# Adding the squares on VectorE, with fewer and later tiny sums, and giving the order of the opening wave of a macaron layer by hand

## The chip, the core and the metric

The kernel runs on one core of one Trainium2 chip. A core has engines that each work through their own instructions in order: TensorE (PE in the profile, with its weight loads as PEld), VectorE (DVE), ScalarE (ACT), GpSimd (POOL), and SyncE (SP), which here only issues DMAs. The metric is the device time in microseconds (us). Three runs of the kernel before gave 2667.14, 2667.64 and 2669.3 us.

## The reference

```
h  = modulate(rms_norm(s, g), shift, scale)          # rms_norm(s) * g * (1 + scale) + shift
s += 0.5 * gate * (silu(h @ w_gate) * (h @ w_up)) @ w_down
```

This half feed-forward step, over 256 latent and 256 context tokens of 2048 features with 5632 hidden features, stands at the beginning and at the end of the layer; attention and a long convolution stand between. The shift, scale and gate of each step are `silu(c) @ w_ada + b_ada`, one vector of 2048 for the latent tokens and one for the context tokens. The convolution's filters come from a small sine network over positions, and are normalised and taken to the frequency domain; they depend on no token. Every large product is made from a high and a low part of each operand, as three products: high x high, high x low, low x high.

## The kernel before

The change lies in the first 170 us. Tokens run along the free axis and features along the partitions, so the input is 16 "d-tiles" of 128 features by 512 tokens (256 of each stream).

**Opening.** SP loads the input as 16 tiles of 256 KB (L547; each holds two d-tiles of one stream). ScalarE squares a tile as it arrives (L592), VectorE squares three of them (L585) and adds neighbours in pairs, and PE multiplies the squares by a matrix of ones (L603), 4 products of 2 columns for each pair and for each of the two last tiles, 36 in all; they are called the tiny sums here. Products of a constant by ones that nobody reads (`keep_awake`, L576) stand ahead of them and between them; an fp32 product of PE is recorded as two passes, so the first `keep_awake(8)` shows as 16. From the sums come 1/rms (L262 to L271), a diagonal matrix of it (L296) and a product that spreads it over the partitions (L297).

**Rows and columns.** Shift and scale of a d-tile are made on PE: a "row" of 16 products by `w_ada` (L174), a copy by ScalarE (L181), two transposes (L183), and on VectorE a reduction (L186) and four operations on single columns (L188, L190). A row needs two loads of 1 MB (`wrow`, L161); the pool holds four such tiles, so that the loads of row d+2 can start when row d has been read.

**Wave.** The normalised input of a d-tile is made by `wave_h`: scale times 1/rms (L622, VectorE), shift (L624, ScalarE, which rounds to the high part), and the low part (L626, VectorE). Three hidden tiles are then accumulated over the 16 d-tiles: a "tile" in the code is the 18 products of one d-tile (L232, L233, L234), 6 for each of the three. Round d holds row d+1, the transposes for d+1, and tile d. Weights of four d-tiles come at a time; their high part is cast by ScalarE (L221), their low part made by VectorE (L225), three of each for rounds 4 to 7, 8 to 11 and 12 to 15. In the kernel before they are cast at the head of rounds 4, 8 and 12.

**Filters.** `filter_spectrum` is a generator that the rounds advance three times each. It makes three sine layers (PE L436; VectorE L438 to L443; ScalarE L445), and then for each of four groups: exponentials (ScalarE, L467), a split of the last weights (L469, L470), the first filter products (PE L474, L475), their products with the exponentials (L476), sums and differences (L481, L482), absolute values (ScalarE, L486), their sum (L488, L489), the normaliser (PE L492, L493, then a reciprocal, L495), the transform (PE L501, VectorE L502 to L507), and two stores that ScalarE's queue issues (L509).

**Order.** A scheduling layer decides the order of each engine from the program and the marks `issue_after` (in `then`), which say behind which instruction another may be placed. What is not marked, it places where it expects it to be ready. At run time each engine's order is fixed. After the wave, 41 more hidden tiles and the rest of the layer follow.

Of the kernel before, what the change touches and what calls it, by code (L numbers as in the profile page):

```python
# [18 lines left out]
P = 128  # L19
# [17 lines left out]
AWAKE = (8, 3, 4)  # L37
# [18 lines left out]
def hybrid_layer_kernel(ctx: ExitStack, tc: tile.TileContext, a):  # L56
# [58 lines left out]
    mod = [[None] * 9, [None] * 9]  # L115
    for c in range(9):
        for i in range(2 if c < 5 else 1):
            mod[i][c] = T(const, (P, KT), f"mod{i}_{c}")
# [58 lines left out]
    def ada_col(d):  # L177
# [9 lines left out]
        for i in range(2):  # L187
            V.scalar_tensor_tensor(mod[i][1][:, d : d + 1], col[:, 0, i : i + 1], bada1[:, d : d + 1], gn[:, 0, d : d + 1],  # L188
                                   op0=ALU.add, op1=ALU.mult)
            V.tensor_add(mod[i][0][:, d : d + 1], col[:, 1, i : i + 1], bada[:, d : d + 1])  # L190
# [221 lines left out]
    def filter_spectrum():  # L412
# [20 lines left out]
        for li in range(3):  # L433
# [13 lines left out]
            if li == 0:  # L447

                mats = U((P, 2, 2, P))
                nc.sync.dma_start(mats, a["fdft"])  # L450
                taps = [load_taps(0)]
# [118 lines left out]
    def keep_awake(n, behind=None, bank=spin):  # L570

        with ExitStack() as order:
# [9 lines left out]
    step = None  # L582
# [4 lines left out]
    for n, t in enumerate(xs[0] + xs[1]):  # L587
        i, sq = n // 8, U((P, 2, L))
        if n in (5, 8, 11):
# [5 lines left out]
        if n < 14 and n % 2 == 0:  # L595
            prior = sq
            continue
        if n < 14:
            step = vector(V.tensor_add, sq, prior, sq)
        for tt in range(2):  # L600
            for j in range(2):
                with tc.issue_after(awake.ins):
                    last = PE.matmul(sums[:, 2 * i + tt, :], sq[:, j, tt * P : (tt + 1) * P], ones[:, 0:2],  # L603
                                     start=(n, tt, j) == (1, 0, 0), stop=(n, tt, j) == (15, 1, 1))
                awake = last
        if n in (3, 7, 11):
            awake = keep_awake(1, awake)
# [7 lines left out]
    with tc.issue_after(spread_mm[-1].ins):  # L615
        ada_row(0, (1,))

# [16 lines left out]
    with tc.issue_after(roots[-1].ins):  # L634
        made = first_hi(0, head)
    with tc.issue_after(made.ins):
        copied, turned_, bank = ada_col(0)
    keep_awake(AWAKE[1], turned_, bank)
    with tc.issue_after(spread.ins):
        made = [first_hi(j, head) for j in range(1, WAVE)][-1]  # L640
    with tc.issue_after(made.ins):
        shifted, lo_last = wave_h(0)
    with tc.issue_after(lo_last.ins):
        for j in range(WAVE):
            first_lo(j, head)
# [9 lines left out]
    def col_on(d):  # L655
        if d < KT:
            ada_col(d)
            wave_h(d)

    firsts = []  # L660
    for d in range(KT):
# [755 lines left out]
```

## Time and profile before

| | us |
|---|---|
| median of three runs | 2667.64 |
| the profiled execution's own time | 2666.05 |
| its span, from the first to the last instruction | 2664.3 |
| PE busy in the span | 2642.3 |
| VectorE busy | 1721.9 |
| ScalarE busy | 939.1 |
| mean granted TensorE clock | 0.996 |

A row of the timeline gives start, duration, engine, line, operation, output <- inputs, sizes, and how many instructions it merges; in brackets stands how long the engine was idle before, and what ended that. In a row of the stage windows stand the stage, its length, the busy time of PE, PEld, DVE, ACT and POOL with their instruction counts, the granted clock as a share of full speed, the busy share of the DMA engines, and GB/s. PE's records overlap, so that its busy time says less than the distance between starts.

### The profile page before, as it was taken

How to read it: one execution, taken by the hardware profiler on the slowest of the kernel's cores; microseconds unless marked ns; L12 is line 12 of the kernel's file. 1: busy time of each engine (PE TensorE's matmuls, PEld its weight loads, DVE VectorE, ACT ScalarE, POOL GpSimd, SP SyncE). 2: the span in 40 equal slices, each digit the busy share in tenths (PEclk: the TensorE clock that was granted, in tenths of full speed). 3: DMA queues.
4: the chain of work that ended last, by engine and by line, in shares of the span. 5: the costliest groups of instructions: out<-in, count | busy, mean ns of one | idle time of the engine just before them, and what ended most of it. 6: DMA issues, size and time to landing. Idle time of an engine off the chain costs nothing.

```text
span 2664.3 us, 32528 instructions
## 1 busy us (share of the span) xinstructions
PE 2642.3 (99%) x12522; PEld 2176.8 (82%) x12522; DVE 1721.9 (65%) x2727; ACT 939.1 (35%) x1236; POOL 7.3 (0%) x19
## 2 busy tenths in 40 slices
PE   9999999999999999999999999999999999999999
PEld 6578888888888888888888988888788888888887
DVE  4779899986596767543434597789765555554444
ACT  3333222222222222222222465457454444444333
POOL 0000000000000000000000000000000000000000
PEclk8999999999999999999999999999999999999999
DMA  9876656665686566622222355335555555556664
GB/s 353 306 270 221 228 211 221 214 228 206 227 294 237 206 226 213 229 95 100 98 95 95 135 174 190 127 121 166 180 176 189 190 189 189 189 190 206 203 200 158
DMA packets 145686, 515.77 MB, mean 194 GB/s; under 512 B 16699, under 2 KB 21756, under 8 KB 141180
## 3 DMA queue, kind: packets, MB, share of 16 engines
q1 hardware_dynamic: 142460, 504.13, 55.1%
q0 software_dynamic: 1296, 4.72, 0.5%
q10 hardware_dynamic: 1776, 4.85, 0.5%
q8 instruction: 98, 1.61, 0.2%
q14 instruction: 56, 0.46, 0.1%
HBM read 509.43 MB, written 4.21 MB: 193 GB/s over the span
## 4 chain that ended last, share of the span: by engine, by line
PE 97%; DVE 1%; DMA 1%; ACT 1%; SPq 0%; issue 0%; DVEq 0%; ACTq 0%
PE pa L232 12%; PE pa L233 12%; PE pa L234 12%; PE pa L1080 10%; PE pa L1081 10%; PE pa L1079 10%; PE pb L232 7%; PE pb L233 7%; PE pb L234 7%; PE pa L240 3%; PE pa L242 2%; PE pa L793 1%; PE pa L794 1%; PE pa L792 1%; PE pb L174 1%; DMA wrow<-in_w_ada_dram 0%
## 5 line engine op out<-in xcount | busy, mean ns | idle before, releaser
L225 DVE TENSOR_TENSOR wlo<-raw,whi 128x1024 fp32r<-128x1024 f32 x639 | 781.4, 1223 | 649.2 <-ACT whi L221 642.8
L221 ACT CAST whi<-raw 128x1024 fp32r<-128x1024 f32 x639 | 672.3, 1052 | 1342.7 <-PE pa L233 485.9
L232 PE MATMUL pa<-u,whi 128*128 128x512 f32 x1376 | 535.3, 392 | 6.6 <-ACT u L624 6.4
L233 PE MATMUL pa<-u,whi 128*128 128x512 f32 x1376 | 536.7, 390 | 0.0
L234 PE MATMUL pa<-u,wlo 128*128 128x512 f32 x1376 | 535.7, 389 | 0.0
L1079 PE MATMUL pa<-whi,u 128*128 128x512 f32 x1060 | 413.9, 391 | 0.0
L1080 PE MATMUL pa<-wlo,u 128*128 128x512 f32 x1060 | 412.8, 390 | 0.2 <-DVE wlo L225 0.2
L1081 PE MATMUL pa<-whi,u 128*128 128x512 f32 x1060 | 412.8, 390 | 0.0
L232 PEld LDWEIGHTS pa<-u,whi 128*128 128x128 f32 x1376 | 258.2, 188 | 65.0 <-ACT u L624 8.4
L233 PEld LDWEIGHTS pa<-u,whi 128*128 128x128 f32 x1376 | 258.5, 188 | 55.0 <-issue 1.2
L234 PEld LDWEIGHTS pa<-u,wlo 128*128 128x128 f32 x1376 | 258.5, 188 | 53.5
L232 PE MATMUL pb<-u,whi 128*128 128x512 f32 (+1 forms) x800 | 298.5, 373 | 0.0
L233 PE MATMUL pb<-u,whi 128*128 128x512 f32 (+1 forms) x800 | 298.1, 373 | 0.0
L234 PE MATMUL pb<-u,wlo 128*128 128x512 f32 (+1 forms) x800 | 297.5, 372 | 0.0
L1081 PEld LDWEIGHTS pa<-whi,u 128*128 128x128 f32 x1060 | 199.0, 188 | 41.4
L1080 PEld LDWEIGHTS pa<-wlo,u 128*128 128x128 f32 x1060 | 199.1, 188 | 41.3 <-DVE wlo L225 0.6
L1079 PEld LDWEIGHTS pa<-whi,u 128*128 128x128 f32 x1060 | 199.0, 188 | 40.8
L137 DVE CUSTOM_DVE_ANT_0 adas<-adaw,crow,mod 128x1024 bf16<-128x1024 f32 x160 | 205.1, 1282 | 17.1 <-DMA adaw<-in_w_adaT_dram 14.1
L137 DVE CUSTOM_DVE_ANT_0 adas<-adaw,crow,cond 128x1024 bf16<-128x1024 f32 x160 | 204.8, 1280 | 15.5 <-DMA adaw<-in_w_adaT_dram 13.8
L232 PEld LDWEIGHTS pb<-u,whi 128*128 128x128 f32 x800 | 150.6, 188 | 27.2 <-issue 0.9
L233 PEld LDWEIGHTS pb<-u,whi 128*128 128x128 f32 x800 | 150.7, 188 | 26.8 <-issue 0.8
L234 PEld LDWEIGHTS pb<-u,wlo 128*128 128x128 f32 x800 | 150.7, 188 | 26.1
(277 smaller groups left out, 2136.1 us busy)
## 6 DMA issues: line engine op xcount, KB each, us to landing
raw<-in_w_up_dram SPq DMA_DIRECT2D x340, 512.0 KB, 3.3
adaw<-in_w_adaT_dram SPq DMA_DIRECT2D x223, 512.0 KB, 4.7
raw<-in_w_dn_dram SPq DMA_DIRECT2D x184, 512.0 KB, 3.4
wrow<-in_w_ada_dram SPq DMA_DIRECT2D x32, 1024.0 KB, 8.3
raw<-in_w_hy_dram SPq DMA_DIRECT2D x32, 512.0 KB, 3.3
raw<-in_w_o_dram SPq DMA_DIRECT2D x32, 512.0 KB, 3.4
raw<-in_w_kv_dram SPq DMA_DIRECT2D x16, 512.0 KB, 3.2
raw<-in_w_q_dram SPq DMA_DIRECT2D x16, 512.0 KB, 3.3
```

The costliest lines, as they stand in the source:

```text
L137: V.tensor_tensor_reduce(out=sc, in0=t, in1=crow[i][:, b * (D // 2) : (b + 1) * (D // 2)], scale=1.0, scalar=mcol if b else bada[:, n : n ...
L174: last = PE.matmul(bank[g : g + 32, 0 : 2 * P], cs[:, k, :], t[:, k8, :], start=k < 4, stop=k >= KT - 4)
L221: S.copy(hi, raw)
L225: V.tensor_sub(lo, raw, hi.bitcast(F32))
L232: PE.matmul(ps, w[0], xx[0], start=start, stop=False)
L233: PE.matmul(ps, w[0], xx[1], start=False, stop=False)
L234: return PE.matmul(ps, w[1], xx[0], start=False, stop=stop)
L240: PE.matmul(ps, w[0], x, start=start, stop=stop)
L242: PE.matmul(ps[:, 0, :], w[1], x[:, 0, :], start=False, stop=False)
L1079: PE.matmul(ps[t], hi, w[0], start=start, stop=False)
L1080: PE.matmul(ps[t], hi, w[1], start=False, stop=False)
L1081: last = PE.matmul(ps[t], lo, w[0], start=False, stop=stop)
```

## The change

1. **Squares.** ScalarE squares 15 tiles, VectorE only tile 14. VectorE adds tiles 0 to 7 into one and 8 to 13 into another. The tiny sums are 16 instead of 36: of the first sum, of the second, and of tiles 14 and 15.
2. **`keep_awake`.** 32 products at the start instead of 8, 14 behind the first tiny sums instead of three single ones, none behind the transposes of d-tiles 0 and 1 (3 and 4 before).
3. **1/rms ahead.** For d-tiles 0 and 1, VectorE multiplies the input by 1/rms beforehand (`times_rs`), and ScalarE applies scale and shift at once (`wave_h_early`); VectorE makes the same again and subtracts the high part.
4. **Columns.** Shift and scale of both streams of a d-tile are written by two operations on two columns instead of four on one.
5. **Order of a round.** Each tile, row and pair of transposes is marked to stand behind the one before: row d+1, the first third of tile d, the transposes, the other two thirds. The filter's products stay unmarked, between them.
6. **Weights.** The casts for rounds 4, 8 and 12 are written behind the thirds of rounds 3, 7 and 11.
7. **Filter loads.** The loads of the first group (`taps`) stand one sine layer later.

```diff
-AWAKE = (8, 3, 4)
+AWAKE = (32, 0, 0, 14)
...
-        if n in (5, 8, 11):
+        if n == 14:
...
-        if n < 14 and n % 2 == 0:
-            prior = sq
+        if n < 14 and n % 8:
+            step = vector(V.tensor_add, acc, acc, sq)
+        if n in (7, 13):
+            sq = acc
+        elif n < 14:
+            acc = acc if n % 8 else sq
             continue
-        if n < 14:
-            step = vector(V.tensor_add, sq, prior, sq)
...
-        if n in (3, 7, 11):
-            awake = keep_awake(1, awake)
+        if n == 7:
+            awake = keep_awake(AWAKE[3], awake)
...
+    def times_rs(d):
+        early[d] = U((P, 2, L))
+        for i in range(2):
+            last = V.tensor_mul(early[d][:, i, :], xd(i, d), rs[:, i, :])
+        return last
+    def wave_h_early(d):
...
+            shifted = S.activation(hi[:, i, :], t[:, i, :], AF.Identity, bias=mod[i][0][:, d : d + 1],
+                                   scale=mod[i][1][:, d : d + 1])
...
+            V.tensor_scalar(t[:, i, :], t[:, i, :], mod[i][1][:, d : d + 1], mod[i][0][:, d : d + 1],
+                            op0=ALU.mult, op1=ALU.add)
+        last = V.tensor_sub(lo, t, hi.bitcast(F32))
...
+    def weights_on(d, j):
+        if d % 4 == 3 and d + 1 < KT:
+            w[j] = weight(None, (P, 4, 2, P), raw=raws[j])
...
+    for d in range(1, KT):
         if d > 1:
-            then(mm, row_on, d + 1)
+            mm = then(mm, row_on, d + 1) or mm
         for j in range(WAVE):
-            if d and d % 4 == 0:
-                w[j] = weight(None, (P, 4, 2, P), raw=raws[j])
-            mm = f1.tile(d, d % 4, w[j], wave[j])
+            mm = then(mm, f1.tile, d, d % 4, w[j], wave[j])
...
+            if j == (1 if d == 1 else 0):
+                mm = then(mm, col_on, d + 1) or mm
+            weights_on(d, j)
+            if (d, j) != (1, 0):
                 next(steps, None)
```

The lines of the changed kernel lie by one or two below those of the kernel before in the generator (its L475 is L474 before); `keep_awake` is L578, the tiny sums L607, the 1/rms products L628, `wave_h_early` L635 to L640, `wave_h` L648 to L652.

**PE, the program's start.** Before, from the seventh row of PE on (`u` the squares or the constant, `pb_171` the sums, `pb_267` row 0):

```order
L576 MATMUL pa_170<-u_74,ones_72 128x256
L603 MATMUL pb_171<-ones_72,u_221 128x2 x4
L603 MATMUL pb_171<-ones_72,u_230 128x2 x4
L576 MATMUL pa_170<-u_74,ones_72 128x256
L603 MATMUL pb_171<-ones_72,u_240 128x2 x4
L603 MATMUL pb_171<-ones_72,u_247 128x2 x4
L603 MATMUL pb_171<-ones_72,u_253 128x2 x4
L174 MATMUL pb_267<-wrow_142,csp_76 32x256 x8
L297 MATMUL pb_277<-sg_276,ones_72 128x512
L174 MATMUL pb_267<-wrow_144,csp_76 32x256 x8
L183 MATMUL pb_267<-ident_67,sg_296 128x128 x2
L576 MATMUL pb_267<-u_74,ones_72 128x256 x3
```

In the changed kernel, from PE's first product on:

```order
L578 MATMUL pa_167<-u_74,ones_72 128x256 x32
L607 MATMUL pb_168<-ones_72,u_201 128x2 x4
L578 MATMUL pa_167<-u_74,ones_72 128x256 x14
L607 MATMUL pb_168<-ones_72,u_243 128x2 x4
L607 MATMUL pb_168<-ones_72,u_264 128x2 x4
L607 MATMUL pb_168<-ones_72,u_270 128x2 x4
L175 MATMUL pb_284<-wrow_139,csp_76 32x256 x8
L297 MATMUL pb_294<-sg_293,ones_72 128x512
L175 MATMUL pb_284<-wrow_141,csp_76 32x256 x8
L184 MATMUL pb_284<-ident_67,sg_321 128x128 x2
```

All 46 idle products now stand ahead of the last 12 tiny sums, and none behind the transposes.

**VectorE in round 4.** Before, the last sine layer (L442, L443), the weights (L225) and the reduction of row 5 (L186):

```order
L442 SCALAR_TENSOR_TENSOR mt_573<-mt_574,mt_573 128x256
L225 TENSOR_TENSOR wlo_636<-raw_468,whi_635 128x1024
L443 TENSOR_SCALAR mt_573<-mt_573 128x256
L225 TENSOR_TENSOR wlo_682<-raw_470,whi_681 128x1024
L626 SCALAR_TENSOR_TENSOR u_594<-sq_595,mod_0_6_83,u_593 128x256
L626 SCALAR_TENSOR_TENSOR u_594<-sq_595,mod_0_7_84,u_593 128x256
L457 TENSOR_TENSOR u_645<-u_582,u_645 64x256
L225 TENSOR_TENSOR wlo_701<-raw_472,whi_700 128x1024
L186 TENSOR_REDUCE col_99<-pb_614 128x4
```

In the changed kernel, at the same place (row 5 is `pb_628`):

```order
L442 SCALAR_TENSOR_TENSOR mt_597<-mt_598,mt_597 128x256
L187 TENSOR_REDUCE col_96<-pb_628 128x4
L442 SCALAR_TENSOR_TENSOR mt_597<-mt_598,mt_597 128x256
L188 SCALAR_TENSOR_TENSOR mod_6_83<-col_96,bada_17_95,cond_78 128x2
L442 SCALAR_TENSOR_TENSOR mt_597<-mt_598,mt_597 128x256
L190 TENSOR_SCALAR mod_6_83<-col_96,cond_78 128x2
L443 TENSOR_SCALAR mt_597<-mt_597 128x256
```

The sine layer's last operations have moved from ahead of row 5's reduction to behind it.

**PE and VectorE at the end of round 7.** PE before, from the end of tile 7 on (`pb_955` is the second group's normaliser, `wrow_905` row 9):

```order
L234 MATMUL pb_294<-u_843,wlo_701 128x512
L174 MATMUL pb_888<-wrow_814,csp_76 32x256 x8
L174 MATMUL pb_888<-wrow_816,csp_76 32x256 x8
L183 MATMUL pb_888<-ident_67,sg_921 128x128 x2
L232 MATMUL pa_289<-u_930,whi_983 128x512
L232 MATMUL pa_290<-u_930,whi_983 128x512
L492 MATMUL pb_955<-u_865,ones_72 128x256
L493 MATMUL pb_955<-u_915,u_165 1x256
L174 MATMUL pb_962<-wrow_905,csp_76 32x256 x8
```

PE in the changed kernel, where row 8 and its transposes stand earlier in round 7 (row 9 is `wrow_901`):

```order
L233 MATMUL pb_311<-u_830,whi_624 128x512
L234 MATMUL pb_311<-u_829,wlo_625 128x512
L493 MATMUL pb_961<-u_861,ones_72 128x256
L494 MATMUL pb_961<-u_931,u_162 1x256
L175 MATMUL pb_968<-wrow_901,csp_76 32x256 x8
```

VectorE there, in the changed kernel, right behind the reduction of row 8 and its two small steps:

```order
L648 SCALAR_TENSOR_TENSOR sq_920<-u_115,mod_6_83,u_166 128x256
L648 SCALAR_TENSOR_TENSOR sq_920<-u_131,mod_6_83,u_166 128x256
L225 TENSOR_TENSOR wlo_928<-raw_789,whi_927 128x1024
L652 SCALAR_TENSOR_TENSOR u_919<-sq_920,mod_6_83,u_918 128x256 x2
L482 TENSOR_TENSOR u_931<-u_861 128x256
L483 TENSOR_TENSOR u_931<-u_861 128x256
L482 TENSOR_TENSOR u_934<-u_863 128x256
L483 TENSOR_TENSOR u_934<-u_863 128x256
L225 TENSOR_TENSOR wlo_944<-raw_791,whi_943 128x1024
L489 TENSOR_TENSOR u_861<-u_861,u_863 128x512
L225 TENSOR_TENSOR wlo_958<-raw_793,whi_957 128x1024
L490 TENSOR_TENSOR u_861<-u_861 128x256
```

PE's normaliser product has moved to the end of round 7, ahead of row 9; what makes its operand (L490) is the last of a chain on VectorE that begins with row 8's reduction and holds all three low parts of the weights.

More of the change, by code (lines that the diff above doesn't have):

```diff
@@ L570, in keep_awake @@
     def keep_awake(n, behind=None, bank=spin):
+        last = behind
         with ExitStack() as order:
@@ L581, in hybrid_layer_kernel @@
     awake = keep_awake(AWAKE[0])
-    step = None
+    step, acc = None, None
     def vector(do, *args):
@@ L653, in row_on @@
             return row
[L655 to L661, printed above, removed]
+    def weights_on(d, j):
+        if d % 4 == 3 and d + 1 < KT:
+            w[j] = weight(None, (P, 4, 2, P), raw=raws[j])
+    for j in range(WAVE):
+        mm = f1.tile(0, 0, w[j], wave[j]) if j == 0 else then(mm, f1.tile, 0, 0, w[j], wave[j])
+    with tc.issue_after(shifted.ins), tc.issue_after(lo_last.ins):
+        for j in range(2):
+            first_hi(j, rest)
+            first_lo(j, rest)
+        scaled = times_rs(1)
```

80 lines of the change are left out of this document (39 added, 41 removed).

## The prediction

> **What bounds the kernel now.** I read the page first, then busy time and clock by stages, then PE's waits, then the timeline of the stage that waits.
>
> ```profile
> 12.70:26.20 13.50, 13.28 (x64) 10.23 (x67) 3.38 (x10) 4.55 (x9) 0.00 (x0) 0.50 1.03 407
> ...
> 57.00:60.30 3.30, 3.20 (x19) 1.74 (x20) 0.00 (x0) 0.37 (x1) 0.00 (x0) 0.50 1.02 422
> ...
> 101.40:108.10 6.70, 5.25 (x33) 2.52 (x37) 4.41 (x8) 0.91 (x2) 0.00 (x0) 0.50 0.48 198
> ...
> 167.40:2664.20 2496.80, 2487.91 (x11510) 2072.79 (x11510) 1615.87 (x2446) 874.26 (x1121) 0.00 (x0) 1.00 0.54 185
> ```
>
> From 167.4 us on PE is busy for 2487.9 of 2496.8 us at the full clock. The change touches nothing behind that, so it can move the end only by moving the moment at which the wave ends. Ahead of it the clock is granted at half in three stretches: around the tiny sums, and behind 57 and 101 us.
>
> ```profile
> PE pa L232 <- ACT u L624: 6.4, 5, 3.3
> PE pb L174 <- DMA wrow<-in_w_ada_dram: 2.5, 1, 2.5
> PE pb L183 <- ACT sg L181: 1.6, 3, 0.6
> ```
>
> Up to 250 us PE's products wait 6.4 us for the wave's input (L624), 2.5 us once for row 4's load, and 1.6 us for copies. These, the half clock and the opening are what can be won.
>
> ```profile
> 1.25 5.94 PE L576 MATMUL pa<-u,ones 128*128 128x256 f32 x16 [1.25 <-POOL u L91]
> 8.41 1.05 PE L603 MATMUL pb<-ones,u 128*128 128x2 f32 x8 [0.43 <-DVE u L255]
> ...
> 16.84 5.12 PE L603 MATMUL pb<-ones,u 128*128 128x2 f32 x24
> ...
> 24.05 2.08 PE L297 MATMUL pb<-sg,ones 128*128 128x512 f32 x2 [0.22 <-DVE sg L296]
> ...
> 28.30 0.17 DVE L186 TENSOR_REDUCE col<-pb 128x4 f32<-128x16 f32 x1 [4.31 <-PE pb L183]
> 28.53 1.56 PE L576 MATMUL pb<-u,ones 128*128 128x256 f32 x6 [0.34 <-DVE col L186]
> ...
> 30.39 0.97 PE L232 MATMUL pa<-u,whi 128*128 128x512 f32 x3 [0.30 <-ACT u L624]
> ...
> 38.10 1.99 PE L576 MATMUL pb<-u,ones 128*128 128x256 f32 x8
> 39.79 0.77 PE L232 MATMUL pa<-u,whi 128*128 128x512 f32 x2
> ...
> 67.84 0.96 PE L232 MATMUL pa<-u,whi 128*128 128x512 f32 x3 [0.94 <-ACT u L624]
> ...
> 72.33 0.61 PE L474 MATMUL pb<-u,u 128*128 128x512 f32 x2
> ...
> 167.47 0.50 PE L232 MATMUL pa<-u,whi 128*128 128x512 f32 x1 [0.15 <-ACT sg L369]
> ```
>
> The marks I use: the tiny sums end at 21.96 (16.84 + 5.12), tile 0 starts at 30.39, tile 1 at 39.79, tile 4 ends at 72.33, and the wave at 167.2, just ahead of the last row. All times below are on this profiled execution's clock.
>
> **The opening.** It gets longer. Eight warm passes of an idle product take 1.99 us and six 1.56, so one takes 0.215. The first 16 took 5.94 where 16 warm ones would take 3.4: about 2.4 us went to a cold start. In the changed kernel 64 passes stand first: 1.25 + 64 x 0.215 + 2.4 = 17.4 us. The first eight tiny passes (1.05 us in the row with the tail of the last, 0.9 apart) bring 18.3, the 28 idle passes 6.0 more, 24.3, the last 24 tiny ones 2.7: 27.0. The additions on VectorE (0.7 us each, following the arrival of the tiles) are done by about 16 and are covered by this. Warm sums do save: 24 passes cost 5.12 at half clock. But they end 5.0 us later than before, because the 46 idle products cost more than the clock returns.
>
> From the end of the sums to the spreading product it took 2.09 us (21.96 to 24.05), so it starts at 29.1 and, warm, takes half of its 2.08. From its end to the reduction it took 2.17 (26.13 to 28.30): 32.3; on VectorE the new 1/rms products and three small low parts stand ahead, five operations of about 0.42 from 30.7 on, so I take 32.7. From reduction to tile 0 it was 2.09; without two column steps and the scaling product (together 0.6) it is 1.5. Tile 0 starts at 34.2, 3.8 later. The next such stretch, tile 0 to tile 1, took 9.40 and loses the same 0.6; the four idle products taken away there were inside this wait. Tile 1 starts at 43.0.
>
> A rule of the Trainium skill bears on this, "TensorE: Matmul & The Clock Gate", in its part on the HAM clock gate: a free-running window of 3.4 us in which PE is busy opens the clock, an idle one halves it. By PE's busy column the 13.50 us stretch above is busy for 13.28 and should have run at the full clock; the row shows 0.50, so tiny sums did not count as busy here, and the measurement decides. By the rule as it reads, the sums before would have cost half and the new opening would lose some 7 us instead of 5.
>
> **Rounds 1 to 4.** From tile 1 to the end of tile 4 it took 32.5 us before. The filter loads now stand behind row 4's, so the 2.5 us wait goes, and with it the half clock of 57.00 to 60.30, which cost 1.65. With the weights cast a round sooner, the 0.94 in the row at 67.84 goes too. 27.4 remain, and tile 4 ends at 70.4, 1.9 us ahead of before. The rows' loads are issued later, too, since row 2 is read later; I keep that for a rival.
>
> **Rounds 5 to 15.** Before, 72.33 to 167.2 held 94.9 us: 5.7 of waits (6.4 less 0.30 and 0.94, and one 0.5 for a copy), 3.35 lost in the half clock of 101.40 to 108.10, and 85.8 of work that stays. If nothing else happened, the wave would end at 156.2. But the new order puts filter products, whose operands come late, where PE can do nothing else: row, tile and transposes stand in line behind them. PE has about 2.9 us of products between the transposes and a round's end (12 at 0.217, the mean of the 11510 in the 167.4 stage, and the transposes).
>
> ```profile
> 50.90 0.17 DVE L186 TENSOR_REDUCE col<-pb 128x4 f32<-128x16 f32 x1 [0.24 <-PE pb L183]
> 51.99 0.28 DVE L443 TENSOR_SCALAR mt<-mt 64x256 f32<-64x256 f32 x1
> ...
> 66.26 0.28 DVE L443 TENSOR_SCALAR mt<-mt 128x256 f32<-128x256 f32 x1
> 67.99 0.36 ACT L181 COPY sg<-pb 128x256 f32<-128x256 f32 x1
> 70.91 0.60 ACT L469 CAST u<-u 128x512 fp32r<-128x512 f32 x1
> ...
> 77.56 0.38 PE L183 MATMUL pb<-ident,sg 128*128 128x128 f32 x2
> 78.05 0.17 DVE L186 TENSOR_REDUCE col<-pb 128x4 f32<-128x16 f32 x1 [1.23 <-PE pb L183]
> 78.14 0.68 DVE L488 TENSOR_TENSOR u<-u,u 128x512 f32<-128x512 f32 x1
> 79.39 0.65 PE L492 MATMUL pb<-u,ones 128*128 128x256 f32 x2
> 79.47 0.88 DVE L622 SCALAR_TENSOR_TENSOR sq<-u,mod,u 128x256 f32<-128x256 f32 x2
> ...
> 87.37 0.69 DVE L502 TENSOR_TENSOR u<-pb,mt 128x512 f32<-128x512 f32 x1 [2.67 <-PE pb L501]
> 88.09 0.42 DVE L503 TENSOR_TENSOR u<-u 128x256 f32<-128x256 f32 x1
> ...
> 90.62 0.88 DVE L626 SCALAR_TENSOR_TENSOR u<-sq,mod,u 128x256 fp32r<-128x256 f32 x2 [0.18 <-ACT u L624]
> ```
>
> End of round 4: transposes to reduction 0.49 (77.56 to 78.05); reduction to the last sine step 1.09, as at 50.90 to 51.99, where the same instructions interleave; from there to the end of the cast L469 5.25 (66.26 to 71.51) less the copy's 0.36, which now stands earlier. That is 6.5 to the first filter product, plus 0.1: PE stands 3.7 us, and 0.3 more for the low part. Before, the sine layer stood ahead of the reduction, and PE came to the same product at 72.33 without a wait.
>
> ```profile
> 115.92 0.82 ACTq L509 DMA_DIRECT2D spec<-u  x2
> ...
> 116.80 0.72 ACT L467 ACTIVATE u<-u,u 128x512 f32<-128x512 f32 x1 [2.00 <-DVE u L507]
> 117.42 0.60 ACT L469 CAST u<-u 128x512 fp32r<-128x512 f32 x1
> ```
>
> End of round 6: the second group's exponentials stand on ScalarE behind the two stores of the first group, and these wait for VectorE's last copies. From the transposes: 0.49, small steps 0.4, L622 0.88, L502 0.69, L626 0.88, two additions of 0.42, overlaps of 0.1 each taken off: 3.9. Stores, two exponentials and the cast: 2.1 (115.92 to 118.02) and 0.6 for the second exponential. PE, with 0.9 of transform products more, has 3.8: it stands 2.9, and 0.3 as above.
>
> ```profile
> L225 DVE TENSOR_TENSOR wlo<-raw,whi 128x1024 fp32r<-128x1024 f32 x639 | 781.4, 1223 | 649.2 <-ACT whi L221 642.8
> L221 ACT CAST whi<-raw 128x1024 fp32r<-128x1024 f32 x639 | 672.3, 1052 | 1342.7 <-PE pa L233 485.9
> ```
>
> End of round 7: VectorE does, between the reduction and the normaliser's operand, 0.4 of small steps, 0.88, three low parts at 1.22, 0.88, four additions of 0.42, and 1.25 from L488 to the product (78.14 to 79.39). With 0.49 ahead and overlaps off, 8.3: PE stands 5.4. This is the price of the weights cast a round sooner: the third low part stands in the chain that PE waits for, and in the kernel before the normaliser had two products and no full round's end ahead of it.
>
> End of round 11: scale 1.3 after the transposes, shift 0.9, a cast of 1.05 (L221), two exponentials 1.3, a cast 0.6: 5.2, PE stands 2.3. Copies held up behind stores and absolute values in rounds 11 and 12: 0.9. Together 15.8 us, against the 5.7 that went.
>
> ```profile
> 53.60:57.00 3.40, 0.96 (x16) 0.31 (x15) 0.88 (x2) 1.73 (x4) 0.00 (x0) 1.00 1.01 392
> 97.90:101.30 3.40, 1.19 (x18) 0.39 (x10) 2.90 (x10) 1.42 (x3) 0.00 (x0) 1.00 0.65 234
> 87.70:91.10 3.40, 1.99 (x10) 1.30 (x8) 3.22 (x14) 1.02 (x3) 0.00 (x0) 1.00 1.04 419
> ```
>
> **The clock behind the stalls.** PE was busy for 0.96 and 1.19 us in the two windows that were followed by half clock, and for 1.99 in one that was not. The three stalls of over 3 us leave such a window more often than not; a fall costs 1.0 to 2.7 us, until a busy window has passed. I take 1.5 each, 4.6. By the skill's rule, that a whole idle window is needed, only the longest would count, and the sum would be 3 us less; the rows above show falls behind windows that were a third busy.
>
> The wave ends at 156.2 + 15.8 + 4.6 = 176.6, 9.4 us later than 167.2. The profiled execution took 2666.05, 1.6 below the median; on the median of 2667.64 that makes 2677.
>
> **The rivals.** 0.2%, or 5.3 us, is about what a measurement of this kernel can tell from no change.
>
> *The stalls do not stand* (the other side). If the chains end within the 2.9 us, PE runs back to back: 9.4 - 15.8 - 4.6 = 11 faster, 2657. For it: L474 came in time before (no bracket at 72.33). Against it: engines run in their fixed order, and the chains' rows add up to 5 to 8 us. It decides at a chain of 2.9 us.
>
> *The stalls stand, the clock holds.* Windows fall so that none is idle enough: 4.8 slower, 2672.4. For it: 1.99 us of work kept the clock; against it: two of the three stalls are longer than the 2.5 us that lost it.
>
> *Only round 7 stalls.* Its chain is the one made of VectorE's work alone; the other three go through ScalarE and could be shorter by what it does ahead. 9.4 less 9.5 and 3.1 is 3 faster, 2664.
>
> *Transfers become the bound.* Rows 3 to 5 are asked for 3 us later while the weights of round 4 arrive. One wait like the 2.5 before, with its half clock, makes 4 more: 2681.
>
> **How the numbers follow.** The forecast has 0.48, the clock that holds 0.17, round 7 alone 0.10, transfers 0.09, no stalls 0.16. The forecast's own range is 2670 (no clock loss, each stall half a microsecond shorter) to 2685 (2.7 each, 1.7 at the opening, each half longer); with round 7 alone it begins at 2664, and about 0.2 lie outside, the case of no stalls above all. Slower by over 0.2%: 0.43 of the forecast, 0.07 of the holding clock, the transfers: 0.59. Within: 0.05, 0.10 and 0.10: 0.25. Faster: 0.16.
>
> **What would show it.** Right: tiny sums ending near 27 at the full clock, tile 0 near 34; no wait for row 4's load; PE idle for 3 to 5 us ahead of the first filter product in rounds 4 and 6 and ahead of the normaliser in round 7, with VectorE busy throughout in the last; half clock behind them; the wave's end near 177. Wrong: these products following the tile without a gap, or sums ending by 22.

## The result and the profile after

The changed kernel took 2686.23 us (median of six runs, 2684.28 to 2686.68) against 2668.47 for the kernel before (six runs): a ratio of 1.0064 with a 95% interval of 1.0051 to 1.0077, 17.8 us slower. The forecast was 9.4 us slower, 2677, with 2685 as its upper end. The sign held, the range missed by 1.2 us, and the size was short by almost half.

In the profiles the distance is 20.3 us at the wave's end and 20.5 us in the span, since the profiled execution of the kernel before lay 2.4 us under its median. Below, as in the prediction, times are those of the profiled executions.

First the changed kernel's PE rows at the forecast's marks. They answer to the marks quoted in the prediction.

```profile
1.25 16.81 PE L578 MATMUL pa<-u,ones 128*128 128x256 f32 x64 [1.25 <-POOL u L91]
...
24.84 2.87 PE L607 MATMUL pb<-ones,u 128*128 128x2 f32 x24
...
29.80 2.08 PE L297 MATMUL pb<-sg,ones 128*128 128x512 f32 x2 [0.23 <-DVE sg L296]
...
36.59 0.73 PE L232 MATMUL pa<-u,whi 128*128 128x512 f32 x2 [1.85 <-ACT u L635]
...
47.81 1.22 PE L232 MATMUL pa<-u,whi 128*128 128x512 f32 x2 [1.28 <-ACT u L635]
```

```profile
80.56 0.49 PE L475 MATMUL pb<-u,u 128*128 128x512 f32 x1 [3.51 <-ACT u L470]
...
102.81 0.80 PE L475 MATMUL pb<-u,u 128*128 128x512 f32 x1 [2.89 <-ACT u L470]
...
119.14 1.22 PE L493 MATMUL pb<-u,ones 128*128 128x256 f32 x2 [5.24 <-DVE u L490]
...
156.09 0.73 PE L475 MATMUL pb<-u,u 128*128 128x512 f32 x2 [1.98 <-ACT u L470]
```

| | before | forecast | changed |
|---|---|---|---|
| tiny sums end | 21.96 | 27.0 | 27.7 |
| tile 0 starts | 30.39 | 34.2 | 36.6 |
| tile 1 starts | 39.79 | 43.0 | 47.8 |
| tile 4 ends (80.56 less the wait of 3.51) | 72.33 | 70.4 | 77.05 |
| the wave ends | 167.2 | 176.6 | 187.6 |

The brackets of the second fence are the forecast waits of rounds 4, 6, 7 and 11: 3.51, 2.89, 5.24 and 1.98 us, where the prediction said 3.7, 2.9, 5.4 and 2.3. The list of what PE waited for in the first 250 us (total, times, longest) adds the small ones:

```profile
PE pb L475 <- ACT u L470: 8.4, 3, 3.5
PE pb L493 <- DVE u L490: 5.2, 1, 5.2
...
PE pb L175 <- DVE u L477: 1.0, 1, 1.0
...
PE pb L476 <- DVE u L471: 0.2, 1, 0.2
```

They sum to 14.8 us; 15.8 were forecast. The wait for row 4's load (2.5 us before) is gone, and so are those for the wave's input from tile 4 on (6.1 of the 6.4 us before).

What the forecast did not have is in the windows. The column behind POOL's is the granted clock:

```profile
27.30:34.10 6.80, 6.21 (x37) 2.00 (x36) 3.10 (x11) 1.99 (x6) 0.00 (x0) 0.50 0.57 210
...
37.50:40.90 3.40, 3.14 (x7) 2.48 (x8) 2.62 (x5) 0.49 (x1) 0.00 (x0) 0.50 0.12 48
...
47.80:51.20 3.40, 3.39 (x10) 1.86 (x14) 3.26 (x7) 0.68 (x1) 1.23 (x3) 0.50 1.00 413
...
81.90:85.30 3.40, 3.40 (x26) 1.45 (x29) 2.90 (x7) 0.77 (x2) 0.00 (x0) 0.50 1.01 404
...
102.40:109.20 6.80, 6.39 (x36) 2.53 (x36) 2.34 (x4) 0.89 (x2) 0.00 (x0) 0.50 0.26 79
...
116.10:122.80 6.70, 3.66 (x26) 1.73 (x27) 4.45 (x5) 0.44 (x1) 0.00 (x0) 0.50 0.01 4
...
157.00:163.80 6.80, 5.78 (x37) 2.65 (x37) 4.38 (x9) 1.53 (x3) 0.00 (x0) 0.50 0.94 320
...
187.70:2684.80 2497.10, 2488.18 (x11510) 2072.89 (x11510) 1616.77 (x2446) 873.06 (x1120) 0.00 (x0) 1.00 0.55 185
```

Apart from the program's start, PE ran at half clock for 37.3 us ahead of the wave's end, in seven stretches; in the kernel before it was 23.5 in three. Behind tile 4 four stretches make 23.7 us. In three of them PE waited (0.4 us ahead of 102.81, 3.0 ahead of 119.14, 1.0 in round 11), so 19.3 us of work ran at half speed, and about 9.6 us were lost there. The forecast had 4.6. The last row, behind the wave, is as before: 2488.2 us busy of 2497.1.

So the 11.0 us between forecast and profile at the wave's end are: 0.7 at the sums, 1.7 from there to tile 0, 2.4 between tiles 0 and 1, 1.8 from tile 1 to the end of tile 4, less 1.0 of waits, and 5.0 of clock behind tile 4 (9.6 less 4.6); 0.4 remain. Apart from the first, the stretches of loss each hold half clock.

### The profile page after: what moved, and what is told of

Its sections match the earlier page's. It is cut to its first block, busy times and chain, and to the rows that moved or that the text cites. A ratio compares the mean times of both kernels' runs of the same rounds, so it can differ in the third digit from the quotient of the medians.

```text
span 2684.8 us, 32551 instructions
## 1 busy us (share of the span) xinstructions
PE 2654.8 (99%) x12538; PEld 2183.4 (81%) x12538; DVE 1725.7 (64%) x2700; ACT 940.5 (35%) x1238; POOL 6.4 (0%) x19
## 4 chain that ended last, share of the span: by engine, by line
PE 97%; DVE 1%; ACT 1%; DMA 1%; issue 0%; SPq 0%; POOL 0%; DVEq 0%; ACTq 0%; POOLq 0%
PE pa L232 12%; PE pa L233 12%; PE pa L234 12%; PE pa L1107 10%; PE pa L1106 10%; PE pa L1105 10%; PE pb L232 7%; PE pb L233 7%; PE pb L234 7%; PE pa L240 3%; PE pa L242 2%; PE pb L175 1%; PE pa L819 1%; PE pa L820 1%; PE pa L818 1%; PE pa L578 1%
## 5 line engine op out<-in xcount | busy, mean ns | idle before, releaser
L225 DVE TENSOR_TENSOR wlo<-raw,whi 128x1024 fp32r<-128x1024 f32 x639 | 782.1, 1224 | 643.4 <-ACT whi L221 635.3
```

Source lines behind the costliest of these rows:

```text
L225: V.tensor_sub(lo, raw, hi.bitcast(F32))
```

## The experiments

My theory after the result (A in most of them): the loss is the waits that were forecast, plus half clock wherever PE is left with too little work. The rivals put it elsewhere: in the order of the rounds alone, in the transfers, or in full engines that would make the operands late wherever PE's products stood. A kernel's median is set against the changed kernel's 2686.23, and its ratio to the kernel before is that of its own comparison. Beside four of them (idle products in the waits, low parts marked, fewer idle products at the start, the first version that beats both) the kernel before took 2666.28 us, about 2.2 less than beside the changed kernel. Measured by their distance to it, these four gained 2.2 us less than their medians say; where that matters, both numbers stand. Rows and windows come from one execution of each kernel.

### The opening undone

The loop over the squares, its 36 tiny sums and the idle products were taken from the kernel before.

```diff
-AWAKE = (32, 0, 0, 14)
+AWAKE = (8, 3, 4)
...
-        if n == 14:
+        if n in (5, 8, 11):
...
-        if n == 7:
-            awake = keep_awake(AWAKE[3], awake)
+        if n in (3, 7, 11):
+            awake = keep_awake(1, awake)
```

> The changed kernel with the squares, the 36 tiny sums and the idle products (8, 3 and 4, and three single ones) of the kernel before; the rounds stay as changed. Theory A, the opening cost more than forecast because PE's clock fell there (tiny sums and idle gaps, with no idle products behind the transposes): tile 0 starts at about 29.8 (36.6 in the changed kernel), tile 1 at about 38.6 (47.8), and the half clock at 47.8 to 51.2 is gone: some 11 us back, 2675. Theory B, the opening costs only what was forecast (3.8 at tile 0, 3.2 at tile 1) and the rest of the loss is made in the rounds: tile 1 comes 3 to 5 us earlier, 2682.

2680.33 us, ratio 1.0044 (1.0031 to 1.0056): 5.9 us back. Tile 0 started at 29.7, tile 1 at 39.8, 8.0 us ahead of the changed kernel's, and the wave ended 8 us sooner. Theory A named tile 0's place to 0.1 us and had tile 1 1.2 too early. The waits in the rounds stayed as they were (3.50, 2.89, 5.24, 1.98). The opening alone costs 6 to 8 us, then, against the 3.2 that the forecast had at tile 1; the rest is made in the rounds.

### The idle products behind the transposes put back

```diff
-AWAKE = (32, 0, 0, 14)
+AWAKE = (32, 3, 4, 14)
```

> The changed kernel with the 3 and 4 idle products behind the transposes of d-tiles 0 and 1 put back (7 products, 3.0 us of PE at the full clock); nothing else. Theory A, without them PE is so little busy before tiles 0 and 1 that the clock is halved: tile 0 starts within 0.3 us of 36.6, its products run at the full clock (1.7 us), and so do those of tile 1 (1.9 us): 2682.6. Theory B, they only filled a wait and the clock depends on something else (the rows, the tiny sums): half clock in tiles 0 and 1 as now, 2686 or up to 1 us more, since they stand in line ahead of the tiles.

2684.14 us, ratio 1.0060 (1.0047 to 1.0072): 2.1 us back by the medians, 3.2 by the wave's end. The windows of this kernel from 30.9 us on (tile 0 starts at 35.6, tile 1 at 45.6):

```profile
30.90:34.30 3.40, 2.25 (x21) 0.89 (x20) 2.14 (x8) 1.47 (x4) 0.00 (x0) 1.00 0.84 318
34.30:41.20 6.90, 6.46 (x36) 4.42 (x39) 3.99 (x8) 2.55 (x4) 0.00 (x0) 1.00 0.32 135
41.20:78.70 37.50, 33.20 (x255) 21.03 (x244) 23.47 (x62) 17.55 (x30) 3.64 (x8) 1.00 0.98 356
```

The half clock in tiles 0 and 1 is gone; both run at the full clock, as theory A said. Of the 3.2 us, 1.0 was there at tile 0 already, because the half clock of the tiny sums had ended at 30.9 and not at 34.1, ahead of the first of the seven products; at most 2.2 are left for them. The prediction had counted their removal at nothing.

But the half clock does not always come without them. The kernel with the low parts marked (below) has the changed kernel's opening, with no idle product behind the transposes. In its profiled execution PE had the full clock from 24.0 to 77.9 us, and tile 0 started at 34.6:

```profile
24.00:77.90 53.90, 44.09 (x338) 27.89 (x340) 31.45 (x84) 22.09 (x40) 3.75 (x8) 1.00 0.88 322
```

```profile
34.58 0.73 PE L232 MATMUL pa<-u,whi 128*128 128x512 f32 x2 [2.02 <-ACT u L637]
```

Tile 1 started at 44.3; the forecast had 34.2 and 43.0. Six kernels here have PE's opening as the changed kernel has it, and in their profiles tile 1 started anywhere from 44.3 to 47.8, the changed kernel last. Five of the six had half clock in tile 0 and four in tile 1. Of the eight kernels with the seven products (the kernel before among them) none had.

### The clock in the rounds held by idle products

Idle products write into the bank of the filter product that PE waits for, ahead of it.

```diff
+                if t == 0 and (7, 7, 0, 5)[q]:
+                    keep_awake((7, 7, 0, 5)[q], at[0], ps.rearrange("p a b -> p (a b)"))
                 PE.matmul(ps, ht, whi, start=True, stop=False)
...
+            if (0, 11, 0, 0)[q]:
+                keep_awake((0, 11, 0, 0)[q], at[0], psn.rearrange("p a b -> p (a b)"))
             PE.matmul(psn[:, 0, :], ones, ab, start=True, stop=True)
```

> The changed kernel with idle products of PE put into its waits: 7 ahead of the first filter products of the first and second group, 11 ahead of the second group's normaliser, 5 ahead of the fourth group's products. Theory A, the half clock in rounds 5, 7, 8 and 12 follows from PE's idleness in the waits ahead of them: the waits' ends move by less than 0.5 us, the half clock goes, and of 9.7 us lost there 7 to 10 come back, 2677 to 2679. Theory B, the clock falls by something else (rows of 32 columns that follow, contention): half clock as now, 2686 to 2688.

2679.40 us, ratio 1.0047 (1.0034 to 1.0061): 6.8 us back by the medians, 4.6 by the distance to the kernel before. From tile 1 to the wave's end there was no half clock at all:

```profile
34.80:38.20 3.40, 3.40 (x7) 2.23 (x8) 3.37 (x6) 1.34 (x2) 0.00 (x0) 0.50 0.35 145
38.20:177.80 139.60, 133.10 (x922) 90.28 (x920) 91.05 (x218) 50.54 (x89) 5.50 (x12) 1.00 0.79 296
```

```profile
PE pb L499 <- DVE u L494: 0.5, 1, 0.5
PE pb L479 <- ACT u L472: 0.5, 1, 0.5
```

At the products that the idle ones stand ahead of, two waits of 0.5 us were left: the real products came when their operands came, hardly later. Rows waited for VectorE 2.9 us in all, where it was 1.0 in the changed kernel. From tile 1 to the wave's end it took 132.2 us instead of 139.9. Theory B is out: the half clock in the rounds follows from PE's idleness. With the idle products of both experiments the kernel should take what the forecast said, or a little more, if clock is what was missed.

> The changed kernel with both sets of idle products: 3 and 4 behind the transposes of d-tiles 0 and 1, and 7, 7, 11 and 5 in the waits for the filter. Nothing of the real work is moved on purpose. Theory A, the clock is what the forecast of 2677 missed: the two effects add (2.1 and 6.8 us by the medians), tile 1 starts at 45.5, no half clock stands behind it up to the wave's end, and the time is 2677 to 2678, the forecast. Theory B, both sets repair the same loss: 2679 to 2680, as with the second set alone.

2676.94 us, ratio 1.0034 (1.0022 to 1.0046): theory A's number. By the medians the two effects add (2.1 and 6.8 make 8.9, measured 9.3); by the distances to the kernel before it is 2.3 and 4.6 against 9.0, so they add to within some 2 us. Its six runs lie within 2.0 us, at a mean clock of 0.999 in each. Its clock from just ahead of tile 0:

```profile
33.90:178.50 144.60, 138.61 (x944) 94.39 (x944) 95.84 (x229) 53.32 (x94) 5.50 (x12) 1.00 0.79 293
```

That it is also the forecast to 0.1 us is partly luck. The forecast had 4.6 us of clock loss in the rounds where this kernel has none, and had tile 1 at 43.0, where it starts at 46.6 here.

### The weights cast at the old place, and the low parts marked

```diff
+            if d % 4 == 0:
+                w[j] = weight(None, (P, 4, 2, P), raw=raws[j])
             mm = then(mm, f1.tile, d, d % 4, w[j], wave[j])
...
-            weights_on(d, j)
```

> The changed kernel with the weights of rounds 4, 8 and 12 cast at the head of these rounds, as before; the order of rows, thirds and transposes stays as changed. Theory A, the three low parts (3 x 1.22 us) stand in VectorE's chain that ends in the normaliser's operand at the end of round 7: the 5.2 us wait at L493 falls to about 1.6 and the half clock behind it (116.0 to 122.9, 1.9 us) goes, 2681, less up to 1 us for waits for the weights at the heads of rounds 4, 8 and 12. Theory B, the chain is late because it begins with row 8's reduction: the wait stays over 4 us, and the casts at the heads add waits of their own: 2686 to 2690.

2685.60 us, ratio 1.0062 (1.0048 to 1.0076), and the wait at the normaliser was 5.25 us. On PE nothing had moved, and on VectorE the low parts of round 8's weights stood where they had stood, since the scheduling layer put them there from the other place as well. So this could not tell the two theories apart, but it shows that writing the casts a round sooner is not what put the low parts into the chain. A mark moves them, with the casts still written at the old place:

```diff
+            if d % 4 == 0:
+                w[j] = weight(None, (P, 4, 2, P), raw=raws[j], behind=summed[-1] if d == 8 else None)
...
-            V.tensor_add(ab, ab, kts[0][:, 1, :])
+            summed.append(V.tensor_add(ab, ab, kts[0][:, 1, :]))
```

> The changed kernel with the low parts of round 8's weights marked to stand behind the addition that ends the second group's absolute sum (the operand of the normaliser). Moving the casts' place in the program had left their place on VectorE as it was, so this marks it. Theory A, the three low parts in the chain are the larger part of the 5.2 us wait at round 7's end: it falls to about 1.8 and its half clock (116.0 to 122.9, 1.9 us) goes or shrinks, some 5 us back, 2681. Theory B, the chain is late by its beginning at row 8's reduction alone: the wait stays over 4 us, 2685 to 2687.

2683.73 us, ratio 1.0068 (1.0052 to 1.0083): 2.5 us back by the medians, only 0.3 by the distance to the kernel before. Its four runs are 2680.64 and 2681.71 at a mean clock of 0.996, and 2685.75 and 2686.27 at 0.993, so the time shows no gain of this edit; the chain does. First VectorE's chain at the end of round 7 in the changed kernel, then in this one (its lines lie two further down):

```profile
111.25 0.17 DVE L187 TENSOR_REDUCE col<-pb 128x4 f32<-128x16 f32 x1 [4.75 <-PE pb L184]
...
112.52 1.22 DVE L225 TENSOR_TENSOR wlo<-raw,whi 128x1024 fp32r<-128x1024 f32 x1
...
115.79 1.22 DVE L225 TENSOR_TENSOR wlo<-raw,whi 128x1024 fp32r<-128x1024 f32 x1
116.92 0.69 DVE L489 TENSOR_TENSOR u<-u,u 128x512 f32<-128x512 f32 x1
117.53 1.22 DVE L225 TENSOR_TENSOR wlo<-raw,whi 128x1024 fp32r<-128x1024 f32 x1
118.66 0.42 DVE L490 TENSOR_TENSOR u<-u 128x256 f32<-128x256 f32 x1
```

```profile
106.86 0.17 DVE L187 TENSOR_REDUCE col<-pb 128x4 f32<-128x16 f32 x1 [5.05 <-PE pb L184]
...
111.72 0.69 DVE L491 TENSOR_TENSOR u<-u,u 128x512 f32<-128x512 f32 x1 [1.11 <-ACT u L489]
112.45 0.42 DVE L492 TENSOR_TENSOR u<-u 128x256 f32<-128x256 f32 x1
112.79 1.22 DVE L228 TENSOR_TENSOR wlo<-raw,whi 128x1024 fp32r<-128x1024 f32 x1
```

From the reduction to the end of the last addition it is 7.8 us with the three low parts and 6.0 without. The wait fell from 5.24 to 3.40, by 1.84, half of the three low parts' 3.66. The other half had lain beside work of ScalarE: without them VectorE stands 1.11 us for the absolute values. Theory A was half right about the wait and wrong about the clock: the half clock behind the normaliser stayed (112.1 to 118.9). The low parts in the chain cost 1.8 us of the wait. The other 3.4 I put down to the product's place in PE's line, a round's end that a reduction, scale, additions and absolute values must reach first; no run tests that alone.

### The filter's products placed later

```diff
+            for _ in range((2, 1, 1, 1)[q]):
+                yield
             for t in range(2):
                 ps, ht = PB((P, 2, L)), hid[:, t * P : (t + 1) * P]
```

> The changed kernel with extra empty steps in the filter's generator ahead of the first filter products of each group (2, 1, 1, 1), so that these products and all behind them are placed one or two thirds of a round later; operands are made where they were. Theory A, the waits of PE in the rounds (3.5, 2.9, 5.2, 2.0, 1.0 us) are there because these products stand in line a third or two ahead of their operands, and the half clock behind them (9.7 us lost) follows from the waits: both nearly go, some 19 us back, 2667. Theory B, VectorE and ScalarE have no room in rounds 4 to 12, so that the operands come late wherever the products stand: the waits move, with about the same sum, 2680 to 2688.

2675.64 us, ratio 1.0032 (1.0019 to 1.0045): 10.6 us back, of 19 expected. The waits that were left:

```profile
PE pb L175 <- DVE mt L499: 3.1, 1, 3.1
PE pb L495 <- DVE u L492: 3.0, 1, 3.0
PE pb L477 <- ACT u L470: 2.9, 1, 2.9
```

In PE's line the products stand further back than the steps say, since a group's extra steps also push back the groups behind it: the first group's moved from the end of round 4 to that of round 5, the second's from round 6 to round 7, and the fourth's from the end of round 11 into round 13. The first and fourth group no longer wait. The second group's products do (2.9 us: their exponentials now stand on ScalarE behind the three casts of round 7), its normaliser too (3.0), and a row waits 3.1 us until VectorE has read the normaliser's bank (L499). Theory A held for the first and fourth group, theory B for the second. In this profile tile 1 started 2.0 us sooner than in the changed kernel, which the edit did not do; from there to the wave's end it took some 131 us instead of 139.9.

### The marks undone

Only a row stays marked behind the tile before it.

```diff
-            mm = then(mm, row_on, d + 1) or mm
+            then(mm, row_on, d + 1)
         for j in range(WAVE):
-            mm = then(mm, f1.tile, d, d % 4, w[j], wave[j])
+            mm = f1.tile(d, d % 4, w[j], wave[j])
...
-                mm = then(mm, col_on, d + 1) or mm
+                col_on(d + 1)
```

> The changed kernel with the thirds of a tile and the transposes unmarked again from d-tile 1 on, so that only a row stands behind the tile before it; opening, weights and loads stay as changed. Theory A, the marks put the filter's products in line ahead of their operands: the waits at the first filter products and the normaliser (13.6 us in the changed kernel) fall to 4 or less, and the stretch from tile 1 to the wave's end falls from 140 us to about 125 (it was 127.7 in the kernel before, with 4.2 us of a load's wait and its clock in it): 2671. Theory B, the waits come with the other edits (weights a round sooner, later start of the wave): they stay over 10 us, 2683 to 2688.

2678.95 us, ratio 1.0040 (1.0026 to 1.0054): 7.3 us back. The waits of this kernel:

```profile
PE pb L493 <- DVE u L490: 4.6, 2, 2.3
PE pa L232 <- ACT u L650: 4.2, 3, 2.1
...
PE pb L184 <- ACT sg L182: 2.8, 5, 0.6
```

The filter's waits fall from 13.6 to 4.6 us, near theory A's number, but the wave's input (4.2) and the copies of rows (2.8) are waited for instead, and the wave from tile 1 on takes 134.4 us where A had 125. So the marks do put the filter's products ahead of their operands, and without them a good part of the wait returns as the one that the kernel before had.

### Fewer idle products at the start

```diff
-AWAKE = (32, 0, 0, 14)
+AWAKE = (22, 3, 4, 4)
```

> The changed kernel with 22, 3, 4 and 4 idle products in place of 32, 0, 0 and 14: fewer ahead of the tiny sums, and some behind the transposes of d-tiles 0 and 1. Theory A, the sums were held up by idle products alone, their squares being ready by 15.6: the sums end at about 19.1 (27.7 in the changed kernel), tile 0 starts at about 27.5 (36.6), tile 1 at about 37.5 (47.8), 10 us back, 2676. Theory B, the transfers of the rows set the opening: the first row's product waits for its load, tile 0 starts at 30 or later and later rows wait for loads, 2680 or more.

2677.44 us, ratio 1.0040 (1.0026 to 1.0053): 8.8 us back by the medians, 6.6 by the distance to the kernel before.

```profile
16.30 2.74 PE L607 MATMUL pb<-ones,u 128*128 128x2 f32 x24
...
27.49 0.73 PE L232 MATMUL pa<-u,whi 128*128 128x512 f32 x2
...
37.52 0.81 PE L232 MATMUL pa<-u,whi 128*128 128x512 f32 x2
```

The sums end at 19.0, tile 0 starts at 27.5 and tile 1 at 37.5: theory A to a tenth. No row waited for a load. With these idle products the 16 sums put tile 1 2.3 us ahead of where both the kernel before and the 36 sums of the first experiment had it (39.8). So what cost time in the opening were the idle products ahead of the sums, and half clock in tiles 0 and 1; this run changes both at once and does not divide the gain between them.

On this kernel I also undid 1/rms ahead, so that d-tiles 0 and 1 are made as the others are:

```diff
-        shifted, lo_last = wave_h_early(0)
+        shifted, lo_last = wave_h(0)
...
-    shifted, lo_last = then(copied, wave_h_early, 1)
+    shifted, lo_last = then(copied, wave_h, 1)
```

> The changed kernel with 22, 3, 4 and 4 idle products and without 1/rms ahead for d-tiles 0 and 1 (both made as the other d-tiles are). Theory A, that edit is worth what the kernel before's rows say, the scaling ahead of ScalarE's step: tile 0 starts 0.3 to 0.6 us later after its transposes and tile 1 the same after its own, 2677.4 + 1 = 2678.4. Theory B, the new form costs as much as it saves, since VectorE makes scale and shift again for the low part: tile 0's low-part products no longer wait 0.4, the same time within 0.5 us, 2677.4.

2678.64 us, ratio 1.0037 (1.0024 to 1.0050), 1.2 us above 2677.44 by the medians, 0.7 nearer to the kernel before by the distance, and within the spread of either. It stays open: the spreading product waited 2.5 us for its operand instead of 1.1, and half clock fell at another place (18.7 to 25.5 instead of 20.7 to 24.1); from transposes to tile it took 0.2 us more at tile 0 and the same at tile 1, and the 0.44 us wait for the low part was gone.

### A version that beats both

Fewer idle products, the low parts of round 8 marked, and empty steps of (2, 2, 2, 1):

> The three together: 22, 3, 4 and 4 idle products, extra empty steps ahead of the filter's products (2, 2, 2, 1), and the low parts of round 8's weights marked behind the first group's sum. Theory A, opening and waits are the whole loss and both can be undone within the changed kernel: 10 us back from the opening, and of the 16 us of waits and the 9.7 of clock in the rounds some 14: 2662, less than the kernel before. Theory B, what was taken from one place comes back at another (loads of rows, VectorE's chains at other rounds): 2668 to 2676.

2657.96 us, ratio to the kernel before 0.9965 (0.9953 to 0.9978): 28 us under the changed kernel, and 8.3 under the kernel before, measured beside it at 2666.28. The windows from the sums' end to the wave's:

```profile
20.80:24.20 3.40, 3.03 (x14) 1.08 (x18) 0.61 (x2) 0.92 (x3) 0.00 (x0) 0.51 1.01 417
24.20:156.40 132.20, 125.10 (x891) 81.74 (x884) 92.01 (x223) 54.13 (x97) 5.62 (x12) 1.00 0.89 338
156.50:2656.40 2499.90, 2490.77 (x11516) 2075.09 (x11514) 1618.74 (x2456) 873.49 (x1118) 0.00 (x0) 1.00 0.55 185
```

The wave ends at 156.4, and behind 24.2 us PE has the full clock. So a kernel with the order by hand and the 16 sums can beat the kernel before, once the idle products and the filter's products stand elsewhere. How much each of the three edits gives here was not measured apart. One more step in the same direction gave nothing more:

```diff
-AWAKE = (22, 3, 4, 4)
+AWAKE = (20, 3, 4, 3)
...
         last = ada_row(0, (0,))
+    last = keep_awake(2, last)
```

> The version that beat the kernel before, with 20, 3, 4 and 3 idle products and two more between the first half of row 0 and the spreading product, where PE waited 1.1 us. Theory A, the sums end at 17.8 (19.1), all that follows comes 1.3 us sooner, and the half clock at 20.8 to 24.2 goes (1 us): 2655.5. Theory B, the clock falls in the tiny sums all the same and the two idle products stand in line: 2657 to 2659.

2658.18 us, ratio 0.9962 (0.9949 to 0.9974), the same. Tile 0 came at 25.3, 2.2 us sooner, and the half clock of 20.8 to 24.2 went; but rows waited 2.4 us behind VectorE's reading of filter products and half clock came at 143.1 to 146.5, and the wave ended at 156.4 as well.

## Why the prediction was right and wrong

**The waits: right.** The places of the four large ones, what each stands behind, and their sum (15.8 forecast, 14.8 measured) held. The 0.9 for copies in rounds 11 and 12 did not come; a row's wait for VectorE (1.0) took its place in the sum by luck. Of the 5.4 at the normaliser the cause was right in part: the prediction called it the price of the weights cast a round sooner, beside the product's new place. The low parts are 1.8 of it, and the casts at the old place did not take even that away.

**What went: right.** The wait for row 4's load and those for the wave's input behind tile 1 are gone. Transfers did not become the bound, and of the other rivals none came: the stalls stood, not in round 7 alone, and the clock did not hold.

**The clock behind the stalls: the right mechanism, too small a term.** The step that failed is "I take 1.5 each, 4.6". It measured about 9.6. The prediction had a better row in hand: 101.40:108.10 at 0.50 is a fall of 6.70 us, 3.35 of it lost, and three of the four falls were of that length. Why a second half-clock window had to pass stays open: in the changed kernel the first window of all three falls holds the end of a wait or another wait, but in the kernel with the opening undone the fall at 94.5 was as long (to 101.3), though PE's wait had ended at 94.42. Nor did I count the wait of round 11, which lost the clock with 2.0 us of waiting.

**The opening at the full clock: wrong.** Two steps failed. "The four idle products taken away there were inside this wait" is true of the time that they took, but with them and the three behind the other transposes the clock holds: in the changed kernel PE had half clock for 3.4 us in tile 0 and in tile 1, 1.7 us lost in each, and with all seven put back it had none there. And the 24 last tiny sums were taken as warm to the end of the row and spreading product behind them, although the prediction's own first row had PE at half clock while it was busy with tiny sums; 1.7 us at tile 0 went that way. Neither loss is certain: the kernel with the low parts marked has the same opening and had no half clock there in its profiled execution, and its tile 0 started 0.4 us behind the forecast's. So the forecast took the best outcome of this opening for the only one. All six runs of the changed kernel have the mean clock of its profiled one, 0.993.

**The range.** Its upper end allowed 1.7 us more at the opening and 2.7 of clock at each of three stalls. Both were passed (4.8 us late at tile 1, about 9.6 of clock in the rounds), and in both places most of it is half clock.

The prediction weighed the Trainium skill's page "TensorE: Matmul & The Clock Gate", Part 1: The HAM clock gate, by which the clock halves after a window without work. In the changed kernel it halved behind a window with 1.64 us of work in 3.4, and behind one with 1.12. The measurement decides, as it did in the prediction, against the page. The same part says that the window runs free of the program, so that one kernel's clock differs from run to run; that agrees with the traces here: with the opening's instructions in the same order, the first half clock lasted from 27.3 to 34.1 in the changed kernel and from 27.5 to 30.9 in the kernel with the casts at their old place, and tile 0 came at 36.6 and 35.6; in the kernel with the low parts marked there was none from 24.0 to 77.9, and tile 0 came at 34.6.

## What to carry to other kernels

Before counting a filler product as free, ask what the clock does without it: a wait costs its length and then half of all that runs until the clock is back, here two thirds as much again (14.8 us of waits and about 9.6 us behind them). A fixed order needs each product marked behind the moment at which its operand can be ready, not behind its neighbour; where a generator fills the gaps, moving the products back by a round or more in PE's line gave more (10.6 us) than any other single edit tried here. A mark moves an instruction, the place of its line may not: look at the order first. And one profile shows one place of the clock's windows: the same opening put tile 1 anywhere between 44.3 and 47.8 here.

## What the runs showed of the hardware

In these traces the clock's threshold lies near half a window. On the 3.41 us grid on which the granted clock changes, I took PE's busy time in each window at the full clock between 5 us and 190 us, in 13 traces, windows with tiny sums apart. Every one of 36 windows with under 1.46 us of work was followed by half clock. Of 21 with 1.49 to 2.04 us, nine were. Of those above, none. Five of these windows, three of the changed kernel (followed by half clock, by full, by half) and two of the one with the filter later (both by full):

```profile
44.40:47.80 3.40, 1.64 (x16) 0.52 (x8) 0.96 (x5) 1.51 (x4) 0.67 (x2) 1.00 0.77 234
75.10:78.50 3.40, 1.95 (x9) 1.28 (x7) 2.72 (x8) 2.73 (x5) 1.75 (x4) 1.00 0.89 262
78.50:81.90 3.40, 1.12 (x3) 0.55 (x3) 0.77 (x2) 2.53 (x5) 0.00 (x0) 1.00 1.05 335
```

```profile
145.90:149.30 3.40, 1.49 (x28) 0.94 (x32) 3.22 (x6) 0.00 (x0) 0.00 (x0) 1.00 0.63 208
98.10:101.50 3.40, 1.92 (x9) 1.24 (x7) 3.40 (x6) 3.15 (x5) 0.00 (x0) 1.00 0.98 351
```

Tiny sums of two columns count for little: in the changed kernel the window from 23.9 to 27.3 is full of them by the busy column (3.40 of 3.40 us), with four idle passes at its beginning, and half clock followed; in the kernel with the filter later one with six such passes and 19 sums was followed by full clock.

What brings the full clock back cannot be read from the busy column either. The least busy window at half clock that was followed by full clock held 2.70 us of work, but this one, of the kernel with the opening undone, is full and was followed by half clock:

```profile
94.50:97.90 3.40, 3.40 (x12) 1.42 (x16) 2.03 (x4) 0.63 (x1) 0.00 (x0) 0.50 0.29 110
```

In it the four first filter products start 0.72 us apart, where the products of tile 0 at half clock in the changed kernel start 0.43 us apart; whether that is the reason is not shown.
